# Weights' parts ahead of what is traced behind them, selection paced by VectorE's queue, recurrence spread, branch sums and keys in swapped tiles

## The chip, the cores and the metric

The kernel runs on one core of a Trainium2 chip. The metric is the device time of one execution in microseconds (us). Engines are called PE (TensorE, matrix products), ACT (ScalarE), DVE (VectorE), POOL (GpSimd) and SP (SyncE, which issues the weight loads).

## The reference, cut to what matters

Two layers work on 512 tokens of width 1024. All arithmetic is float32. One layer:

```python
h = rms_norm(x, g_pre_mix); proj = h @ w_in
q, k, v, qi, ki, wi, xr, gr, zu, zv, gate_logits = jnp.split(proj, offsets, axis=-1)
# rope on q, k, qi, ki
y_a = dsa_attention(q, k, v, qi, ki, wi)      # scores of an indexer, top_k = 128 keys a query, softmax
y_b = rg_lru(causal_depthwise_conv(xr, conv_w, conv_b), ...) * jax.nn.gelu(gr)
y_c = chunked_spatial_gating(jax.nn.gelu(zu), rms_norm(jax.nn.gelu(zv), g_gmlp_v), w_spatial, b_spatial)
branch = jnp.einsum('nbsw,nwd->nbsd', jnp.stack([y_a, y_b, y_c]), w_branch)
merged = jnp.einsum('bsnd,nbsd->bsd', jax.nn.sigmoid(gate_logits), branch)
x = x + rms_norm(merged @ w_out, g_post_mix)
f = jnp.square(jax.nn.relu(rms_norm(x, g_pre_ffn) @ w_ffn_up)) @ w_ffn_down
x = x + rms_norm(f, g_post_ffn)
ple = (p_i @ w_ple) * jax.nn.sigmoid(x @ w_ple_gate)
x = x + rms_norm(ple, g_post_ple)
```

In `rg_lru`, with r and i sigmoids of block products of the input: `a = exp(-8 r softplus(-lambda))`, the input is `sqrt(1 - a*a) * (i * x)`, and the state is the scan `h[t] = a[t] h[t-1] + input[t]`.

## The kernel before

Everything is kept as [128 partitions x 512 tokens] tiles, features on the partitions. A float32 product is made of three passes: each operand is split into a high part (`hi`, `xh`, `wh`) and the rest (`lo`, `xl`, `wl`), and PE adds hi*hi, lo*hi and hi*lo (`mm3`, `gemm` at L306 with its matmuls on L313 to L315). A product over 1024 features is 8 x 3 matmuls of 512 columns.

The weights stream through the core in 512 KB blocks. `prep()` (L233) takes the next block: SP loads it into `wr` (three buffers), ACT casts it to `wh` (L244), DVE subtracts to get `wl` (L245). `wh` and `wl` have four buffers each, and `getw()` runs `prep()` three blocks ahead of the product. The second half of a product done in halves (`gemm_halves`) calls `prep()` itself after each eviction. `gemm_arriving` (matmuls on L371) multiplies while the normalised activations are still being made: `x_tiles` makes them tile by tile, with a scaling (L496 or L498), an addition to the residual `X` (L499, on DVE or POOL in turn), the high part `xh` on ACT (L509) and `xl` on DVE (L519). `Stats` gathers squares (L407 on ACT, L413 on POOL), PE sums them (L423), DVE and POOL make the reciprocal root (L442, L443) and PE spreads it (L449). At the very start DVE and ACT also make the tables of the rotary embedding (L133 to L161, one sine on L154), which PE transposes (L164).

Each engine works through its instructions in order. The order within an engine is set by a scheduler at build time from the order in which the code emits them, from the data dependences, and from order-only edges that the code adds. A model clock (`clk`, advanced by `tick()` after each matmul triple) decides when deferred pieces and tasks are emitted. Tasks are generators in queues: selection (`idxq`), recurrence (`recq`), attention (`attq`). `behind_products(fn)` ties what `fn` emits behind the last matmul emitted so far.

In the stretch of the gate logits and branch products (about 150 to 240 us in layer 1, 1050 to 1145 in layer 2) four things share DVE: the weights' `wl`, the selection rounds (`select`, L724: MAX on L730, MATCH_REPLACE on L732, 16 rounds for each block of queries, then a threshold on L736 to L744), the recurrence (L876: Exp L881, Tanh L882, a square on POOL L884, a product on DVE L885, Sqrt L890, products on POOL L893 and L896, the scan L895) and the gates (L853 on DVE, the Tanh L854 on ACT) with the branch sums (L913, L915, L916). The sums `MA` lie in slots M0 to M7, which earlier hold recurrence inputs (`GG`, `XC`), and the keys `KK` lie in the big slots K0 and K1.

Of the kernel before, what the change touches and what calls it, by code (L numbers as in the profile page):

```python
# [8 lines left out]
F32 = mybir.dt.float32  # L9
F32R = mybir.dt.float32r  # L10
# [3 lines left out]
ALU = mybir.AluOpType  # L14
# [36 lines left out]
def hybrid_block_kernel(ctx, tc, xT, pT, pos, vec, bsp, freq, w_in, w_tok, w_lru, w_sp, w_br, w_out, w_up, w_dn, w_ple, w_gate, out, depth=DEPTH, dbg=None):  # L51
# [40 lines left out]
    PICK = 1.7  # L92
    WARM = 120
# [139 lines left out]
    def prep():  # L233
        i = nprep[0]
        nprep[0] += 1
        key, src = order[i]
        raw = wp.tile([128, 1024], F32, tag="wr", name=nm("wr"), bufs=3)
        nc.sync.dma_start(raw, src)
        if key[0] == "sp":
            r3 = raw.rearrange("p (g t) -> p g t", g=8)  # L240
            G.affine_select(out=r3, in_=r3, compare_op=ALU.is_ge, fill=0.0, base=0, pattern=[[0, 8], [1, 128]], channel_multiplier=-1)
        hi = wp.tile([128, 1024], F32R, tag="wh", name=nm("wh"), bufs=NWB)
        lo = wp.tile([128, 1024], F32R, tag="wl", name=nm("wl"), bufs=NWB)
        A.copy(hi, raw)  # L244
        V.tensor_sub(lo, raw, f32v(hi))  # L245
        prepared[key] = (hi, lo)

# [31 lines left out]

    def run_later(force=False):  # L280
        while later:
            later.sort(key=lambda e: e[:2])
            if not force and later[0][0] > clk[0]:
                return
            later.pop(0)[2]()
# [15 lines left out]
    def tick(us):  # L301
        clk[0] += us
        run_later()
        run_tasks()
# [244 lines left out]
    for l in range(depth):  # L549
# [174 lines left out]
        def select(t, sc):  # L724
# [3 lines left out]
            for r in range(TOPK // 8):  # L728
                m8 = small(8, "m8", 4)
                V.max(m8, (sc if r == 0 else wk)[:, :n])  # L730
                if r < TOPK // 8 - 1:
                    V.match_replace(wk[:, :n], m8, (sc if r == 0 else wk)[:, :n], -3.0e38)  # L732
                yield 0.8 + 1.1 * t
# [127 lines left out]
        for j in range(4):  # L861
# [7 lines left out]
            r, i = tmp(), tmp()  # L869
# [8 lines left out]
        def recurrence():  # L878
            for j in range(4):
                a, s = slot(f"B{j}"), slot(f"B{4 + j}")  # L880
                A.activation(a, Rg[j], AF.Exp, scale=nsp8[:, j:j + 1])  # L881
                A.activation(s, Rg[j], AF.Tanh, scale=sp8[:, j:j + 1])  # L882
                q = tmp()
                G.tensor_mul(q, a, a)  # L884
                V.scalar_tensor_tensor(s, q, 1.0, s, op0=ALU.add, op1=ALU.mult)  # L885
                AS.append((a, s))
                yield 1.5
            yield 3.0
            for j in range(4):
                A.activation(AS[j][1], AS[j][1], AF.Sqrt)  # L890
            for j in range(4):
                a, s = AS[j]
                G.tensor_mul(s, s, XC[j][0])  # L893
                hh = tmp()
                V.tensor_tensor_scan(hh, a, s, 0.0, ALU.mult, ALU.add)  # L895
                G.tensor_mul(hh, hh, GG[j])  # L896
                yh, yl = slot(f"B{j}", F32R), slot(f"B{4 + j}", F32R)
                split(hh, yh, yl)
                YB.append((yh, yl))
                yield 4.0  # L900
# [5 lines left out]
        MA = [None] * 8  # L906

        def branch(n, d, w, y, th):
            ps = bank()
            gemm(ps, w, y, 4, c0=(d % 2) * 128)  # L910
            if n == 2:
                MA[d] = slot(f"M{d}")
# [16 lines left out]
        KK = [slot("K0", F32R, True), slot("K1", F32R, True)]  # L929
# [4 lines left out]
        def attention(j):  # L934

            q2, ql = Q[j]
            kk = KK[0][:, j], KK[1][:, j]
# [97 lines left out]
        for j in range(4):  # L1035
# [12 lines left out]
            turn_later(TURN, lambda f=rope(proj(f"k{j}")), j=j: stacked(f, KK[0][:, j], KK[1][:, j]))  # L1048
# [7 lines left out]
        mh = [slot("K0", F32R, True), slot("K1", F32R, True)]  # L1056
        ml = [slot("V0", F32R, True), slot("V1", F32R, True)]
        M = []
        for d in range(8):
# [3 lines left out]
            hi, lo = mh[d // 4][:, d % 4], ml[d // 4][:, d % 4]  # L1063
# [4 lines left out]
        Y = [slot(f"M{d}") for d in range(8)]  # L1068
# [190 lines left out]
```

## Time and profile before

| | |
|---|---|
| median of 3 runs | 1830.21 us (1828.61 to 1830.43) |
| the profiled execution | 1830.5 us, span 1828.8 us, mean granted clock 0.994 |
| busy: PE, DVE, ACT, POOL | 1793.8, 1169.1, 796.0, 364.4 us |
| PE waits: for `wl` in products, for `xl` in arriving products | 10.5 us (6 times), 8.0 us (9 times) |
| L244 casts, L245 subtractions | 303 each, mean 1050 and 1275 ns |

A matmul of 512 columns starts 0.227 us after the one before it when nothing is awaited, though its record lasts 0.39 us, because its end is modelled. The granted clock is given as a share of the full one. Idle time is put down to the instruction that ended it.

### The profile page before, as it was taken

The numbers are of one execution on the slowest core, as the hardware profiler recorded it, in microseconds if no ns is written. First come the engines' busy times: TensorE is split into PE (matmuls) and PEld (weight loads), VectorE is DVE, ScalarE is ACT, GpSimd is POOL, SyncE is SP. The second block draws the span as 40 slices with busy tenths as digits, with TensorE's granted clock in tenths as the row PEclk, the third lists the DMA queues.
The fourth block names the chain that finished last, engine by engine and source line by source line (L and its number), as shares of the span: only waits on it lengthen the run. The fifth ranks groups of instructions, "written<-read, shape, count | busy, mean of one in ns | idle before, by whom it ended". The sixth has DMA issues, their size and how long they took to land.

```text
span 1828.8 us, 22863 instructions
## 1 busy us (share of the span) xinstructions
PE 1793.8 (98%) x8798; PEld 1503.6 (82%) x8798; DVE 1169.1 (64%) x1939; ACT 796.0 (44%) x1288; POOL 364.4 (20%) x292
## 2 busy tenths in 40 slices
PE   8999999999999999999999999999999999999997
PEld 7887788888888888888888877888889888888886
DVE  6888997756385253533687989977564753544345
ACT  5556336654443232223546463465544432222233
POOL 3513222300230000003455141232004100000033
PEclk9999999999999999999999999999999999999998
DMA  5312322222222232332222223222222322223321
GB/s 163 100 68 87 106 95 82 69 93 81 93 86 100 92 104 92 104 104 92 88 72 102 73 83 99 99 86 70 81 93 81 104 93 95 102 92 104 104 81 58
DMA packets 49678, 167.77 MB, mean 92 GB/s; under 512 B 6048, under 2 KB 8864, under 8 KB 49568
## 3 DMA queue, kind: packets, MB, share of 16 engines
q1 hardware_dynamic: 47376, 163.64, 26.7%
q10 hardware_dynamic: 2192, 2.67, 0.4%
q8 instruction: 69, 1.13, 0.3%
q14 instruction: 41, 0.34, 0.1%
HBM read 164.19 MB, written 2.10 MB: 91 GB/s over the span
## 4 chain that ended last, share of the span: by engine, by line
PE 84%; DVE 7%; issue 3%; POOL 3%; ACT 3%; DMA 0%; SPq 0%; ACTq 0%; POOLq 0%; DVEq 0%
PE ps L313 24%; PE ps L315 24%; PE ps L314 24%; PE ps L606 5%; PE ps L371 4%; DVE wl L245 1%; PE ps L983 1%; DVE tmp L732 1%; PE ps L969 1%; DVE m L730 1%; PE ps L697 1%; POOL sacc L413 1%; POOL X L499 1%; DVE xl L519 1%; PE ps L683 1%
## 5 line engine op out<-in xcount | busy, mean ns | idle before, releaser
L244 ACT CAST wh<-wr 128x1024 fp32r<-128x1024 f32 x303 | 317.9, 1050 | 464.8 <-PE ps L315 380.8
L314 PE MATMUL ps<-xh,wl 128*128 128x512 f32 (+1 forms) x1296 | 496.8, 383 | 10.5 <-DVE wl L245 10.5
L245 DVE TENSOR_TENSOR wl<-wr,wh 128x1024 fp32r<-128x1024 f32 x303 | 385.6, 1275 | 185.8 <-ACT wh L244 185.4
L313 PE MATMUL ps<-xh,wh 128*128 128x512 f32 (+1 forms) x1296 | 503.6, 389 | 0.0
L315 PE MATMUL ps<-xl,wh 128*128 128x512 f32 (+1 forms) x1296 | 496.7, 383 | 0.0
L314 PEld LDWEIGHTS ps<-xh,wl 128*128 128x128 f32 x1296 | 244.8, 189 | 56.5 <-DVE wl L245 13.0
L413 POOL TENSOR_TENSOR sacc<-sacc,tmp 128x256 f32<-128x256 f32 (+1 forms) x99 | 108.4, 1096 | 895.8 <-issue 584.5
L315 PEld LDWEIGHTS ps<-xl,wh 128*128 128x128 f32 x1296 | 244.3, 189 | 48.2
L313 PEld LDWEIGHTS ps<-xh,wh 128*128 128x128 f32 x1296 | 244.5, 189 | 46.0 <-issue 1.9
L315 PE MATMUL ps<-V,wh 128*128 128x512 f32 (+1 forms) x528 | 195.4, 370 | 0.0
L313 PE MATMUL ps<-K,wh 128*128 128x512 f32 (+1 forms) x432 | 158.2, 366 | 0.0
L314 PE MATMUL ps<-K,wl 128*128 128x512 f32 (+1 forms) x432 | 157.8, 365 | 0.0
L315 PE MATMUL ps<-B,wh 128*128 128x512 f32 x336 | 131.0, 390 | 0.0
L313 PE MATMUL ps<-A,wh 128*128 128x512 f32 x320 | 125.0, 391 | 0.2 <-ACT A L384 0.2
L314 PE MATMUL ps<-A,wl 128*128 128x512 f32 x320 | 124.6, 389 | 0.0
L1118 DVE TENSOR_TENSOR M<-M,ps 128x512 f32<-128x512 f32 x48 | 33.0, 688 | 141.1 <-PE ps L315 141.1
L1106 DVE TENSOR_TENSOR tmp<-ps,R 128x512 f32<-128x512 f32 x64 | 43.8, 690 | 111.1 <-PE ps L315 109.8
L315 PEld LDWEIGHTS ps<-V,wh 128*128 128x128 f32 x528 | 99.5, 188 | 16.9
L371 PE MATMUL ps<-xl,wh 128*128 128x256 f32 (+1 forms) x264 | 87.2, 330 | 8.5 <-DVE xl L519 8.0
L313 PEld LDWEIGHTS ps<-K,wh 128*128 128x128 f32 x432 | 81.4, 189 | 13.2
L314 PEld LDWEIGHTS ps<-K,wl 128*128 128x128 f32 x432 | 81.5, 189 | 13.1
L371 PE MATMUL ps<-xh,wh 128*128 128x256 f32 (+1 forms) x264 | 85.6, 324 | 1.4 <-ACT xh L509 1.3
(235 smaller groups left out, 2729.1 us busy)
## 6 DMA issues: line engine op xcount, KB each, us to landing
wr<-in_w_in_dram SPq DMA_DIRECT2D x95, 512.0 KB, 3.3
wr<-in_w_up_dram SPq DMA_DIRECT2D x64, 512.0 KB, 3.3
wr<-in_w_dn_dram SPq DMA_DIRECT2D x64, 512.0 KB, 3.3
wr<-in_w_br_dram SPq DMA_DIRECT2D x24, 512.0 KB, 3.3
wr<-in_w_tok_dram SPq DMA_DIRECT2D x16, 512.0 KB, 3.3
wr<-in_w_out_dram SPq DMA_DIRECT2D x16, 512.0 KB, 3.3
wr<-in_w_gate_dram SPq DMA_DIRECT2D x16, 512.0 KB, 3.3
X<-in_xT_dram SPq DMA_DIRECT2D x8, 256.0 KB, 5.4
```

The lines of the kernel that those rows point to most:

```text
L244: A.copy(hi, raw)
L245: V.tensor_sub(lo, raw, f32v(hi))
L313: PE.matmul(ps, wh, xh, start=start, stop=False)
L314: PE.matmul(ps, wl, xh, start=False, stop=False)
L315: PE.matmul(ps, wh, xl, start=False, stop=stop)
L371: PE.matmul(pss[o][:, r], (h3, l3, h3)[m][:, q], xs[q][m // 2][:, r], start=q == 0 and m == 0, stop=q == KT - 1 and m == 2)
L413: G.tensor_add(sacc[:, r], sacc[:, r], self.q[r.start, r.stop])
L499: (G if d in on_g else V).tensor_add(X[d][:, r], X[d][:, r], ys[d][:, r])
L519: V.scalar_tensor_tensor(lo, x, g[:, d:d + 1], f32v(hi), op0=ALU.mult, op1=ALU.subtract)
L606: PE.matmul(ps, x, w, start=k == 0 and i == 0, stop=k == KT - 1 and i == 2)
L1106: V.tensor_mul(t, ps, R)
L1118: V.tensor_add(F[d], F[d], ps)
```

## The change

It has four parts. (1) `weights_first()` runs at the head of each `prep()`: every ACT and DVE instruction emitted since the last `prep()` gets an order-only edge behind that `prep()`'s last cast and last subtraction. (2) A selection round no longer yields a fixed time; `count()` keeps an account of DVE's queue from the sizes of the emitted instructions, and a round is emitted when `vector_free()` finds the queue empty at the model clock. (3) The recurrence makes the Tanh before the Exp, which works in place in the B slots; the square goes from POOL to ACT; square roots, scans and the final splits are tied behind products and spread by longer yields. (4) The branch sums go to the big slots K0 and K1, the keys to M0 to M7, the merged high parts to the M slots, and Y to K0 and K1.

```diff
--- before.py
+++ after.py
@@ -90,6 +90,7 @@
     ATT = 13
     TURN = 7
     PICK = 1.7
+    SLACK = 0.3
     WARM = 120
     FIRST = [0, 1, 4]
 
@@ -231,6 +232,7 @@
     nget = [0]
 
     def prep():
+        weights_first()
         i = nprep[0]
         nprep[0] += 1
         key, src = order[i]
@@ -244,6 +246,21 @@
         A.copy(hi, raw)
         V.tensor_sub(lo, raw, f32v(hi))
         prepared[key] = (hi, lo)
+        ins = nc.cur_bb.bb.instructions
+        parts[:] = [len(ins)] + [next(i.name for i in reversed(ins) if i.engine == e) for e in ENG]
+
+    ENG = (mybir.EngineType.Activation, mybir.EngineType.DVE)
+    parts = []
+
+    def weights_first():
+
+        if not parts:
+            return
+        for i in nc.cur_bb.bb.instructions[parts[0]:]:
+            for e, name in zip(ENG, parts[1:]):
+                if i.engine == e:
+                    tc.add_manual_dep(i, name, mybir.DependencyInfo(mybir.DependencyClass.NoSync, mybir.DependencyReason.SCHED_ONLY), reason="weights first")
+        parts.clear()
 
     def getw(key, ahead=LA):
         assert order[nget[0]][0] == key, (order[nget[0]][0], key)
@@ -276,6 +293,26 @@
 
     def turn_later(us, fn):
         defer(us, lambda: behind_products(fn))
+
+    dve = [0.0, 0]
+
+    def vector_free():
+
+
+        count()
+        return dve[0] <= clk[0] + SLACK
+
+    def count():
+        ins = nc.cur_bb.bb.instructions
+        for i in ins[dve[1]:]:
+            n = 1
+            for _, c in (list(i.outs[0].ap)[1:] if i.outs and hasattr(i.outs[0], "ap") else ()):
+                n *= c
+            if i.engine == mybir.EngineType.DVE:
+                dve[0] = max(dve[0], clk[0]) + 0.08 + n * 0.00118
+            elif i.engine == mybir.EngineType.Pool:
+                dve[0] = max(dve[0], clk[0]) + n * 0.0012
+        dve[1] = len(ins)
 
     def run_later(force=False):
         while later:
@@ -299,6 +336,7 @@
                         q["act"].remove(a)
 
     def tick(us):
+        count()
         clk[0] += us
         run_later()
         run_tasks()
@@ -730,7 +768,9 @@
                 V.max(m8, (sc if r == 0 else wk)[:, :n])
                 if r < TOPK // 8 - 1:
                     V.match_replace(wk[:, :n], m8, (sc if r == 0 else wk)[:, :n], -3.0e38)
-                yield 0.8 + 1.1 * t
+                yield 0.6
+                while not vector_free():
+                    yield 0.3
             thr = m8[:, 7:8]
             gt, cnt = tmp(), small(1, "cnt", 4)
             V.tensor_scalar(gt[:, :n], sc[:, :n], thr, None, op0=ALU.is_gt, op1=ALU.add, accum_out=cnt)
@@ -866,7 +906,7 @@
             pr, pi = bank(), bank()
             mm3(pr, w3[0][:, j], w3[1][:, j], xh, xl, True, True)
             mm3(pi, w3[0][:, 4 + j], w3[1][:, 4 + j], xh, xl, True, True)
-            r, i = tmp(), tmp()
+            r, i = slot(f"B{j}"), tmp()
             A.activation(r, pr, AF.Sigmoid, bias=col(V_BA + j))
             A.activation(i, pi, AF.Sigmoid, bias=col(V_BX + j))
             G.tensor_mul(xc, xc, i)
@@ -877,39 +917,51 @@
 
         def recurrence():
             for j in range(4):
-                a, s = slot(f"B{j}"), slot(f"B{4 + j}")
-                A.activation(a, Rg[j], AF.Exp, scale=nsp8[:, j:j + 1])
-                A.activation(s, Rg[j], AF.Tanh, scale=sp8[:, j:j + 1])
+                a, s = Rg[j], slot(f"B{4 + j}")
+                A.activation(s, a, AF.Tanh, scale=sp8[:, j:j + 1])
+                A.activation(a, a, AF.Exp, scale=nsp8[:, j:j + 1])
                 q = tmp()
-                G.tensor_mul(q, a, a)
+                A.activation(q, a, AF.Square)
                 V.scalar_tensor_tensor(s, q, 1.0, s, op0=ALU.add, op1=ALU.mult)
                 AS.append((a, s))
-                yield 1.5
+                yield 2.5
             yield 3.0
-            for j in range(4):
-                A.activation(AS[j][1], AS[j][1], AF.Sqrt)
+
+            def roots():
+                for j in range(4):
+                    A.activation(AS[j][1], AS[j][1], AF.Sqrt)
+
+            behind_products(roots)
+            yield 3.0
             for j in range(4):
                 a, s = AS[j]
                 G.tensor_mul(s, s, XC[j][0])
+                yield 3.0
                 hh = tmp()
-                V.tensor_tensor_scan(hh, a, s, 0.0, ALU.mult, ALU.add)
-                G.tensor_mul(hh, hh, GG[j])
+
+                def scan(hh=hh, a=a, s=s, j=j):
+                    V.tensor_tensor_scan(hh, a, s, 0.0, ALU.mult, ALU.add)
+                    G.tensor_mul(hh, hh, GG[j])
+
+                behind_products(scan)
                 yh, yl = slot(f"B{j}", F32R), slot(f"B{4 + j}", F32R)
-                split(hh, yh, yl)
                 YB.append((yh, yl))
-                yield 4.0
+                turn_later(5.0, lambda hh=hh, yh=yh, yl=yl: split(hh, yh, yl))
+                yield 5.0
 
         recq = {"wait": [recurrence()], "act": [], "max": 1}
         queues.append(recq)
 
 
-        MA = [None] * 8
+        MA, MB = [None] * 8, []
 
         def branch(n, d, w, y, th):
             ps = bank()
             gemm(ps, w, y, 4, c0=(d % 2) * 128)
             if n == 2:
-                MA[d] = slot(f"M{d}")
+                if d % 4 == 0:
+                    MB.append(slot(f"K{d // 4}", F32, True))
+                MA[d] = MB[d // 4][:, d % 4]
                 V.scalar_tensor_tensor(MA[d], th, 1.0, ps, op0=ALU.add, op1=ALU.mult)
             else:
                 V.scalar_tensor_tensor(th, th, 1.0, ps, op0=ALU.add, op1=ALU.mult)
@@ -926,7 +978,7 @@
         finish(recq)
 
 
-        KK = [slot("K0", F32R, True), slot("K1", F32R, True)]
+        KK = [[slot(f"M{4 * s + j}", F32R) for j in range(4)] for s in range(2)]
 
         VV = [slot("V0", F32R, True), slot("V1", F32R, True)]
         Q, YA = [], [None] * 4
@@ -934,7 +986,7 @@
         def attention(j):
 
             q2, ql = Q[j]
-            kk = KK[0][:, j], KK[1][:, j]
+            kk = KK[0][j], KK[1][j]
             vv = VV[j // 2]
             L = {}
 
@@ -1045,7 +1097,7 @@
 
             turn_later(TURN, q_split)
             Q.append((q2, ql))
-            turn_later(TURN, lambda f=rope(proj(f"k{j}")), j=j: stacked(f, KK[0][:, j], KK[1][:, j]))
+            turn_later(TURN, lambda f=rope(proj(f"k{j}")), j=j: stacked(f, KK[0][j], KK[1][j]))
             if j == 0:
                 finish(idxq)
             defer(ATT, lambda j=j: add_task(attq, attention(j)))
@@ -1053,19 +1105,19 @@
 
         TH = [gate(0, d) for d in range(8)]
         finish(attq)
-        mh = [slot("K0", F32R, True), slot("K1", F32R, True)]
         ml = [slot("V0", F32R, True), slot("V1", F32R, True)]
         M = []
         for d in range(8):
             if d % 2 == 0:
                 w = getw(("br", l, 0, d // 2))
             branch(0, d, w, YA, TH[d])
-            hi, lo = mh[d // 4][:, d % 4], ml[d // 4][:, d % 4]
+            hi, lo = slot(f"M{d}", F32R), ml[d // 4][:, d % 4]
             split(MA[d], hi, lo, scale=0.5)
             M.append((hi, lo))
 
 
-        Y = [slot(f"M{d}") for d in range(8)]
+        yb = [slot("K0", F32, True), slot("K1", F32, True)]
+        Y = [yb[d // 4][:, d % 4] for d in range(8)]
         st = Stats()
         st2 = Stats()
 
```

The lines of the file move with it: L245 becomes L247, L496 and L499 become L534 and L537, L519 becomes L557, L730 and L732 become L768 and L770, L885 becomes L925.

The order of DVE at the start of the program, before and then with the change. `wl_413` to `wl_482` are the first four weights after the first product, `tmp_436` to `tmp_466` the rope tables, `xl_27` the last of the first activations:

```order
L160 TENSOR_SCALAR tmp_466<-tmp_436 128x4x8
L161 COPY tmp_466<-tmp_436 128x4x8
L245 TENSOR_TENSOR wl_422<-wr_419,wh_421 128x1024
L245 TENSOR_TENSOR wl_431<-wr_428,wh_430 128x1024
L245 TENSOR_TENSOR wl_482<-wr_479,wh_481 128x1024
L442 TENSOR_SCALAR sm_502<-ps_497 128x4
```

```order
L557 SCALAR_TENSOR_TENSOR xl_27_252<-X_233,vec_79,xh_26_251 128x512
L247 TENSOR_TENSOR wl_413<-wr_410,wh_412 128x1024
L247 TENSOR_TENSOR wl_422<-wr_419,wh_421 128x1024
L247 TENSOR_TENSOR wl_431<-wr_428,wh_430 128x1024
L134 CAST sm_434<-posi 128x4
L247 TENSOR_TENSOR wl_482<-wr_479,wh_481 128x1024
L139 TENSOR_TENSOR tmp_436<-sm_434,fq 128x32
L159 MEMSET tmp_446 128x512
```

The table instructions, which ended ahead of `wl_422`, now begin behind `wl_482`.

The order of DVE at the boundary from the mix to the feed-forward part of layer 1, before and then with the change. The three `wl` are the first weights of the feed-forward product; the other lines are those of `x_tiles`, and `sm` is a variance:

```order
L245 TENSOR_TENSOR wl_4534<-wr_4531,wh_4533 128x1024
L496 TENSOR_TENSOR M_866_4220<-M_866_4220,ps_4553 128x256
L499 TENSOR_TENSOR X_226<-X_226,M_866_4220 128x256
L496 TENSOR_TENSOR M_867_4221<-M_867_4221,ps_4553 128x256
L245 TENSOR_TENSOR wl_4572<-wr_4569,wh_4571 128x1024
L519 SCALAR_TENSOR_TENSOR xl_13_238<-X_226,vec_79,xh_12_237 128x256
L496 TENSOR_TENSOR M_868_4222<-M_868_4222,ps_4553 128x256
L499 TENSOR_TENSOR X_228<-X_228,M_868_4222 128x256
L519 SCALAR_TENSOR_TENSOR xl_15_240<-X_227,vec_79,xh_14_239 128x256
L496 TENSOR_TENSOR M_869_4223<-M_869_4223,ps_4553 128x256
L245 TENSOR_TENSOR wl_4607<-wr_4604,wh_4606 128x1024
L442 TENSOR_SCALAR sm_4656<-ps_4653 128x2
```

```order
L247 TENSOR_TENSOR wl_4530<-wr_4527,wh_4529 128x1024
L247 TENSOR_TENSOR wl_4568<-wr_4565,wh_4567 128x1024
L247 TENSOR_TENSOR wl_4603<-wr_4600,wh_4602 128x1024
L534 TENSOR_TENSOR K_872_4222<-K_872_4222,ps_4549 128x256
L537 TENSOR_TENSOR X_226<-X_226,K_872_4222 128x256
```

The subtractions stood between the tiles and now stand ahead of the first one; ACT's casts stand ahead of its `xh` likewise.

The order of DVE in the gate stretch of layer 1, around the `wl` that PE waits for at 177 us (`wl_1707` before, `wl_1708` with the change):

```order
L885 SCALAR_TENSOR_TENSOR B_341_1683<-tmp_1686,B_341_1683 128x512
L730 MAX m_357_1732<-tmp_1678 128x8
L732 MATCH_REPLACE tmp_1678<-m_357_1732,tmp_1678 128x384
L885 SCALAR_TENSOR_TENSOR B_355_1720<-tmp_1723,B_355_1720 128x512
L730 MAX m_363_1761<-tmp_1678 128x8
L885 SCALAR_TENSOR_TENSOR B_359_1739<-tmp_1742,B_359_1739 128x512
L853 TENSOR_TENSOR tmp_1751<-ps_1691,R_284 128x512
L732 MATCH_REPLACE tmp_1678<-m_363_1761,tmp_1678 128x384
L730 MAX m_372_1800<-tmp_1678 128x8
L732 MATCH_REPLACE tmp_1678<-m_372_1800,tmp_1678 128x384
L245 TENSOR_TENSOR wl_1707<-wr_1704,wh_1706 128x1024
```

```order
L965 SCALAR_TENSOR_TENSOR K_342_1690<-tmp_1626,ps_1662 128x512
L770 MATCH_REPLACE tmp_1658<-m_340_1681,tmp_1658 128x384
L247 TENSOR_TENSOR wl_1702<-wr_1699,wh_1701 128x1024
L768 MAX m_341_1687<-tmp_1658 128x8
L925 SCALAR_TENSOR_TENSOR B_338_1669<-tmp_1672,B_338_1669 128x512
L770 MATCH_REPLACE tmp_1658<-m_341_1687,tmp_1658 128x384
L247 TENSOR_TENSOR wl_1708<-wr_1705,wh_1707 128x1024
L893 TENSOR_TENSOR tmp_1747<-ps_1692,R_284 128x512
L925 SCALAR_TENSOR_TENSOR B_353_1714<-tmp_1717,B_353_1714 128x512
L925 SCALAR_TENSOR_TENSOR B_355_1732<-tmp_1735,B_355_1732 128x512
```

Between the weight before it and that subtraction stood three recurrence products, a gate product and six selection instructions; now one recurrence product and two selection instructions stand there.

## Rows read from the trace of the kernel before

**Rows 1.** The page, part 1: busy time, share of the span, instructions.

```profile
PE 1793.8 (98%) x8798; PEld 1503.6 (82%) x8798; DVE 1169.1 (64%) x1939; ACT 796.0 (44%) x1288; POOL 364.4 (20%) x292
```

**Rows 2.** PE in time, 177 to 185 us: start, duration, instruction, [idle <-releaser].

```profile
177.16 0.39 PE L313 MATMUL ps<-xh,wh 128*128 128x512 f32 x1
180.82 0.79 PE L314 MATMUL ps<-xh,wl 128*128 128x512 f32 x1 [3.28 <-DVE wl L245]
...
184.27 0.39 PE L313 MATMUL ps<-xh,wh 128*128 128x512 f32 x1
```

**Rows 3.** PE's waits, 170:225, then 1075:1125 us: total, times, longest.

```profile
PE ps L314 <- DVE wl L245: 5.3, 3, 3.3
...
PE ps L314 <- DVE wl L245: 5.1, 3, 3.2
```

**Rows 4.** Windows: busy time (instructions) of PE, PEld, DVE, ACT, POOL; clock, DMA.

```profile
180.80:184.10 3.30, 3.28 (x8) 2.60 (x9) 2.97 (x6) 3.28 (x5) 2.12 (x2) 0.50 0.53 161
1084.20:1088.40 4.20, 4.20 (x12) 3.36 (x13) 3.87 (x6) 4.19 (x6) 3.06 (x3) 0.62 0.39 125
912.00:935.10 23.10, 19.57 (x140) 17.15 (x139) 20.62 (x42) 12.74 (x32) 17.97 (x21) 1.00 0.14 48
```

**Rows 5.** DVE in time, 176 to 181 us.

```profile
179.55 1.22 DVE L245 TENSOR_TENSOR wl<-wr,wh 128x1024 fp32r<-128x1024 f32 x1
```

**Rows 6.** ACT in time, 170 to 176 us.

```profile
172.35 1.03 ACT L244 CAST wh<-wr 128x1024 fp32r<-128x1024 f32 x1
```

**Rows 7.** Line L885, both layers: duration ns min/median/max, first and last start.

```profile
L885 DVE SCALAR_TENSOR_TENSOR B<-tmp,B x8: 666/1589/1768, 168.3 to 1080.0; 128x512 f32<-128x512 f32 x8
```

**Rows 8.** DVE in time, 24 to 36 us.

```profile
24.19 0.18 DVE L138 TENSOR_TENSOR tmp<-sm,fq 128x32 f32<-128x32 f32 x1
24.42 0.48 DVE L158 MEMSET tmp<- 128x512 f32 x1
...
27.16 0.25 DVE L147 TENSOR_SCALAR tmp<-tmp 128x32 f32<-128x32 f32 x2
...
29.33 0.18 DVE L161 COPY tmp<-tmp 128x32 f32<-128x32 f32 x1
32.16 2.36 DVE L245 TENSOR_TENSOR wl<-wr,wh 128x1024 fp32r<-128x1024 f32 x2 [2.66 <-ACT wh L244]
35.02 1.23 DVE L245 TENSOR_TENSOR wl<-wr,wh 128x1024 fp32r<-128x1024 f32 x1 [0.50 <-ACT wh L244]
```

**Rows 9.** ACT in time, 31 to 35 us.

```profile
31.08 2.00 ACT L244 CAST wh<-wr 128x1024 fp32r<-128x1024 f32 x2 [2.27 <-issue]
...
33.94 1.05 ACT L244 CAST wh<-wr 128x1024 fp32r<-128x1024 f32 x1
```

**Rows 10.** PE in time, 32 to 33 us.

```profile
32.20 1.03 PE L164 MATMUL ps<-ident,tmp 128*128 128x128 f32 x8
```

**Rows 11.** DVE in time, 496 to 504 us.

```profile
496.86 0.41 DVE L496 TENSOR_TENSOR M<-M,ps 128x256 f32<-128x256 f32 x1
...
502.16 1.71 DVE L245 TENSOR_TENSOR wl<-wr,wh 128x1024 fp32r<-128x1024 f32 x1
```

**Rows 12.** ACT in time, 500 to 502 us.

```profile
500.60 1.05 ACT L244 CAST wh<-wr 128x1024 fp32r<-128x1024 f32 x1
```

**Rows 13.** PE in time, 499 to 527 us.

```profile
499.76 0.28 PE L371 MATMUL ps<-xh,wh 128*128 128x256 f32 x1
...
526.24 0.48 PE L313 MATMUL ps<-xh,wh 128*128 128x512 f32 x1
```

**Rows 14.** PE's waits, 495 to 527 us: total, times, longest.

```profile
PE ps L371 <- DVE xl L519: 0.9, 2, 0.5
PE ps L371 <- DVE wl L245: 0.4, 1, 0.4
```

**Rows 15.** DVE in time, 908 to 910 us.

```profile
908.99 0.47 DVE L498 SCALAR_TENSOR_TENSOR B<-B,gp,ps 128x256 f32<-128x256 f32 x1
```

**Rows 16.** ACT in time, 912 to 914 us.

```profile
912.73 1.04 ACT L244 CAST wh<-wr 128x1024 fp32r<-128x1024 f32 x1
```

## The prediction

> **What bounds the kernel now.** I read the page first: TensorE (PE) is busy for 98% of the span [rows 1], so the end moves only where PE stands idle or runs slowly. The next view was PE's waits by stretch. In the gate and branch stretch of each layer PE waits three times for the low half `wl` of a weight, 5.3 us in layer 1 and 5.1 us in layer 2 [rows 3]. PE's timeline shows the worst of these: after the matmul at 177.16 us the next starts at 180.82, and the eight starts up to 184.27 come 0.43 us apart where 0.23 is usual [rows 2]. The windows give the clock there: 0.50, the 1.2 GHz level, directly after that idle, and 0.62 over the matching window of layer 2 [rows 4].
>
> Why is `wl` late? Its cast on ScalarE (ACT) ends at 172.35 + 1.03 = 173.4 us [rows 6], but VectorE (DVE) makes the subtraction only at 179.55 [rows 5]. DVE was not waiting for the weight. It worked through selection rounds, recurrence steps and a gate product that stood ahead of it, which is the third order excerpt above. So DVE's order sets this stall, and the change rewrites exactly that order.
>
> **What the stall costs today.** A stall costs its idle time, plus 0.16 us because a 0.39 us record is followed by the next start after 0.23, plus about 0.1 us on the next matmul. Layer 1: 5.3 + 3 x 0.16 + 0.2 for idle, and for the low clock eight starts in 3.45 us instead of 8 x 0.227 = 1.82, so 1.6. That is 7.6 us. Layer 2: 5.1 + 0.7, and twelve starts in 4.20 us instead of 2.72, so 1.5; together 7.3 [rows 2 to 4]. **The most that can be won here is 15 us.**
>
> **Part 1, weights first, in the gate stretch.** In the new order nothing of the selection or the recurrence stands between cast and subtraction except what DVE is already doing. Cast to 173.4, then even behind the longest recurrence product, 1.77 us [rows 7], the subtraction of 1.22 [rows 5] ends at 176.4; PE wants it at 177.16 + 0.23 = 177.4. The stall and its low clock go. The same work still has to be done by DVE, only later, so what is late next would be a subtraction that waits on its cast while a searched block is owed. I charge 0.75 us per layer for that, between 0 (everything on time) and 3 (about the two smaller stalls of a layer kept). Gain: 15.0 - 1.5 = **13.5 us**.
>
> **Parts 2 to 4.** Pacing the selection by an account of DVE's queue changes when rounds are emitted, not how many. The eight squares that move from POOL to ACT and the table loads that fall from 24 to 18 lie on engines that PE does not wait for here, and ACT is 44% busy [rows 1]. Storing the branch sums in other tiles takes away waits of DVE, not work. I cost all of it at nothing by itself: what covers it is the margin of 1 us or more computed above, and if that is gone the charge of 0.75 grows towards 3. One thing is worth a number. The recurrence product L885 takes 0.67 us at best and 1.59 in the median [rows 7], the long ones beside a square on POOL. With the squares on ACT, 4 x (1.59 - 0.67) = 3.7 us of DVE time per layer come free. The page "SBUF — State Buffer" of the Trainium skill, section "SBUF: two separate sides", says that a VectorE instruction with two SBUF inputs and a GpSimd instruction that reads SBUF exclude each other for a whole instruction. By that rule the 3.7 us are really won; without it none would be; the sum stays the same and only the chance of the third rival below falls.
>
> **Part 1 again, where it was not needed: the start.** The rule holds for every weight. In the new order DVE makes four subtractions before it begins the rope tables; before, it did the tables first (first order excerpt). Two of the casts of these weights run at 31.08 to 33.08 [rows 9] and not sooner; I take it that their buffers come free only as PE finishes the first product. The fourth cast, 1.05 us long [rows 9], follows at 33.1 at the earliest. Two subtractions take 32.16 to 34.5 [rows 8], the fourth another 1.2, to 35.7. Only now come the table instructions. They took 0.18 + 0.48 + 0.25 + 0.48 for the head (two memsets among them) and from 27.16 to 29.51 for the rest with the sine [rows 8], 3.7 us; overlaps take off 0.1 and the first table is ready 0.3 before the second. PE's eight transposes of the tables, at 32.20 today [rows 10] and in the same place of PE's order, can start at 35.7 + 3.7 - 0.4 = 39.0. **PE stands 6.8 us** where it stood none. An idle time of 3.3 us was followed by the 1.2 GHz level in layer 1 [rows 2, 4], so I add the same 1.6. Loss **8.4 us**; bounds 5 (casts 2 us sooner and the clock kept) and 9.
>
> **The boundary from mix to feed-forward, in both layers.** Here a weight is cast after each half-product. Before, DVE slipped the normalised activations between the subtractions, beginning at 496.86 [rows 11]. Now all three subtractions precede the first of them (second order excerpt). The third cast cannot run before 500.60 [rows 12], since it follows the eviction of the last half-product. It ends at 501.65, its subtraction at 502.9, so the activations start **6.0 us later**. The first one needs 1.4 us (scale, add, high part) before PE can start: 504.3 instead of 499.76 [rows 13]. From there PE has the same work, 526.24 - 499.76 = 26.5 us [rows 13] less the waits of this stretch, 1.3 [rows 14], and 0.5 for their edges: 24.7. That ends at 529.0, and with 1.6 for the low clock after 4.3 us of idle at 530.6. Loss **4.4 us** each, 8.8 for two. Bounds: 2.4 (DVE's total work decides and the activations catch up) and 6.0 (all of the delay stays).
>
> **The boundary between the layers.** The same shape once: third cast at 912.73 to 913.77 [rows 16], subtraction to 915.0, activations from 915.0 instead of 908.99 [rows 15]. But here PE is fed by DVE anyway: in the 23.1 us after 912 PE is busy for 19.57 and DVE for 20.62 [rows 4], so a permutation of DVE's work costs less than the delay. I take half, **3.0 us**; bounds 0 and 6.
>
> **The sum.** The profiled execution took 1830.5 us (span 1828.8), 0.3 above the median of 1830.2. 1830.5 - 13.5 + 8.4 + 8.8 + 3.0 = 1837.2, so **1837 us**, slower by 0.4%. About 0.2%, 3.7 us, is what a measurement of this kernel can tell from no change: 1826.5 to 1833.9 counts as the same.
>
> **Rivals.**
> *The boundaries hide their delay.* At the three boundaries the products could be bound by DVE's total of work, which the order does not change. Then they cost about 0, and 1830.5 - 13.5 + 8.4 = 1825 us: faster. For it speaks the stretch after 912, where DVE is the busier engine [rows 4]. Against it: in the stretch from 495 PE waits only 1.3 us in all [rows 14], so PE has no slack there to take up a start 4.5 us later. It decides once the three boundaries together cost less than about 1 us. Chance 0.14.
> *The rope tables come in time.* If the buffers of the first weights are free some 5 us earlier, the subtractions end before PE needs the tables; without that loss the sum is 1829 us, no change. Against it: the casts at 31.08 began with no weight missing, after 2.27 us of standing [rows 9], and the buffers depend on PE's matmuls, which the change leaves in place. Chance 0.11.
> *The gate stretch is not relieved.* DVE is nearly full there, and with weights first the postponed searches could end late enough to hold attention or a later subtraction. Half of the gain gone: 1837 + 7 = 1844 us. For it: DVE is busy 2.97 of 3.30 us even in the slow-clock window [rows 4]. Against it: the 3.7 us of L885. Chance 0.15; without those 3.7 us I would give it 0.25.
> That the edges don't take effect is ruled out by the new order itself; the rest, 0.60, is the forecast.
>
> **How the numbers follow.** The forecast's own parts spread by about 5 us to either side, so of its 0.60 some 0.47 lies above 1833.9, 0.12 within the band and 0.01 below. The first rival is split 0.11 faster and 0.03 same, the second 0.04 faster, 0.06 same and 0.01 slower, the third is all slower. Slower: 0.47 + 0.01 + 0.15 = 0.63; same: 0.12 + 0.03 + 0.06 = 0.21; faster: 0.01 + 0.11 + 0.04 = 0.16. The range reaches down into the first rival and up through the third: 1825 to 1845 us; the forecast's own would be 1831 to 1843.
>
> **What the profile after would show.** Right: PE's waits for `wl` in the two gate stretches near zero and the clock full there; one wait of PE of some 6 to 7 us at the table transposes, with the clock at one half after it; in each layer a wait of about 4 us for the first activation of the feed-forward product. Wrong: tables ready near 32 us, PE waits below 1 us at the boundaries, or waits for `wl` still of 1 us and more in the gate stretch.

## The result, and the profile after

| | before | after |
|---|---|---|
| median of 4 runs | 1830.32 us | 1847.18 us (1846.62 to 1847.73) |
| profiled execution, its span | 1830.5, 1828.8 us | 1846.62, 1844.9 us |
| PE busy, mean granted clock | 1793.8 us, 0.994 | 1801.9 us, 0.989 |

The change makes the kernel slower by 0.96%: ratio 1.0096, 95% interval 1.0084 to 1.0108. The direction and most of the places were forecast, but not the size: 1837 us was said, and 1847.2 lies above the range. One execution of run 4 below took 2167.6 us at a granted clock of 0.776 and is left out; in all others the clock is 0.98 or higher. This is what PE waited for after the change, over the whole span (total us, times, longest):

```profile
PE ps L409 <- ACT xh L547: 14.4, 5, 4.4
PE ps L165 <- DVE tmp L162: 6.6, 1, 6.6
PE ps L409 <- DVE xl L557: 3.9, 3, 2.7
PE ps L487 <- POOL rt L481: 2.6, 2, 1.4
...
PE ps L721 <- DVE M L705: 1.4, 2, 1.1
PE ps L644 <- DVE wl L247: 1.3, 2, 0.8
```

The six waits for `wl` in the gate stretches [rows 3] are gone there; L644 is the token product behind them, with 1.3 us in layer 1. New are the rope tables (L165, 6.6 us), the first activations at the three boundaries (L409 for `xh`, the longest 4.4 us), and the first key products (L721).

To see where each microsecond went I compared the start of the same-numbered matmul in both traces; both programs make 8798. "Forecast" is the term of the prediction. The rows of the gate stretch contain the token product behind it.

| stage (matmul numbers) | after minus before, us | forecast |
|---|---|---|
| first products (to 190) | -2.2 | 0 |
| rope tables (190 to 860) | +9.2 | +8.4 |
| gate stretch, layer 1 (860 to 1150) | -5.4 | -6.75 |
| attention, layer 1 (1150 to 2425) | +1.4 | 0 |
| mix to feed-forward, layer 1 (2425 to 2670) | +6.5 | +4.4 |
| boundary between the layers (4150 to 4600) | +4.5 | +3.0 |
| gate stretch, layer 2 (5237 to 5620) | -7.4 | -6.75 |
| attention, layer 2 (5620 to 6780) | +4.9 | 0 |
| mix to feed-forward, layer 2 (6780 to 7000) | +4.8 | +4.4 |
| sum | +16.3 | +6.7 |

**The rope tables.** PE, then DVE, then ACT around 30 us:

```profile
36.82 1.94 PE L165 MATMUL ps<-ident,tmp 128*128 128x128 f32 x8 [6.65 <-DVE tmp L162]
...
38.98 0.63 PE L352 MATMUL ps<-xh,wl 128*128 128x512 f32 x1
39.41 0.63 PE L353 MATMUL ps<-xl,wh 128*128 128x512 f32 x1
```

```profile
29.94 2.36 DVE L247 TENSOR_TENSOR wl<-wr,wh 128x1024 fp32r<-128x1024 f32 x2 [4.23 <-ACT wh L246]
...
32.28 1.22 DVE L247 TENSOR_TENSOR wl<-wr,wh 128x1024 fp32r<-128x1024 f32 x1
33.42 0.18 DVE L139 TENSOR_TENSOR tmp<-sm,fq 128x32 f32<-128x32 f32 x1
...
36.84 0.18 DVE L162 COPY tmp<-tmp 128x32 f32<-128x32 f32 x1
```

```profile
28.85 2.94 ACT L246 CAST wh<-wr 128x1024 fp32r<-128x1024 f32 x3 [7.73 <-PE ps L409]
```

The casts start when PE frees the buffers, as was taken from [rows 9]; they and the arriving products come 2.2 us sooner than in the trace of before. The fourth subtraction ends at 33.5, the tables need until 37.0, and PE stands 6.65 us. Its transposes take 1.94 us instead of 1.03 [rows 10], and from 38.98 on the starts come 0.43 us apart: from 36.8 to 41.5 us the granted clock is 0.50.

**Mix to feed-forward, layer 1.** DVE, POOL and PE:

```profile
504.64 1.22 DVE L247 TENSOR_TENSOR wl<-wr,wh 128x1024 fp32r<-128x1024 f32 x1 [1.65 <-ACT wh L246]
505.78 0.41 DVE L534 TENSOR_TENSOR K<-K,ps 128x256 f32<-128x256 f32 x1
...
513.47 0.16 DVE L480 TENSOR_SCALAR sm<-ps 128x2 f32<-128x2 f32 x1
```

```profile
514.52 0.89 POOL L481 TENSOR_TENSOR rt<-sm,mhalf 128x2 f32<-128x2 f32 x1
```

```profile
507.25 0.58 PE L409 MATMUL ps<-xh,wh 128*128 128x256 f32 x1 [4.36 <-ACT xh L547]
```

The third subtraction precedes the first tile (L534), as in the second order excerpt. PE starts its first arriving product 7.5 us later than before [rows 13], of which 4.4 us are this stall. The variance (L480) now stands behind all tiles of the first half, so POOL makes the root only at 514.52 and PE waits 1.4 us more for it (in L487); the prediction did not count that.

**The keys of layer 2.** PE's timeline, the window behind it (columns as in [rows 4]) and DVE:

```profile
1183.18 0.41 PE L721 MATMUL ps<-M,A 128*128 128x384 f32 x1 [1.08 <-DVE M L705]
1183.90 0.87 PE L721 MATMUL ps<-M,A 128*128 128x384 f32 x3 [0.31 <-DVE M L705]
...
1185.31 0.80 PE L351 MATMUL ps<-B,wh 128*128 128x512 f32 x1
```

```profile
1185.30:1188.80 3.50, 3.50 (x10) 2.78 (x9) 3.50 (x8) 1.72 (x4) 2.20 (x1) 0.52 0.53 159
```

```profile
1181.09 1.23 DVE L247 TENSOR_TENSOR wl<-wr,wh 128x1024 fp32r<-128x1024 f32 x1 [0.19 <-ACT wh L246]
1182.35 1.40 DVE L705 TENSOR_TENSOR M<-tmp,M 64x512 fp32r<-64x512 f32 x2
```

The key tiles `M` (L705) are finished 1.4 us too late, and the clock is at 0.52 for the next 3.5 us. The prediction had no term for this. The wait and the low clock make 3.5 of the 4.9 us that attention loses in layer 2 (by matmul 5660). The other 1.4 us there and the 1.4 us of layer 1 are not the keys: from matmul 1150 to 2425 PE idles for 0.24 us both before and after. In these stretches PE changes between products and attention matmuls 119 and 118 times instead of 109 and 108, as in runs 2 and 4, whose edges reach there too (117 to 119), and in no other run. That this is the cause is not shown.

### The profile page after: what moved, and what is told of

Same layout as the page of the kernel before. It is cut to its first block, busy times and chain, and to the rows that moved or that the text cites. A ratio compares the mean times of both kernels' runs of the same rounds, so it can differ in the third digit from the quotient of the medians.

```text
span 1844.9 us, 22854 instructions
## 1 busy us (share of the span) xinstructions
PE 1801.9 (98%) x8798; PEld 1509.2 (82%) x8798; DVE 1152.2 (62%) x1939; ACT 790.2 (43%) x1290; POOL 348.8 (19%) x284
## 4 chain that ended last, share of the span: by engine, by line
PE 59%; DVE 7%; issue 2%; ACT 1%; POOL 1%; ACTq 0%; POOLq 0%; DVEq 0%
PE ps L351 17%; PE ps L353 17%; PE ps L352 17%; PE ps L409 4%; DVE tmp L770 1%; PE ps L644 1%; DVE wl L247 1%; DVE m L768 1%; PE ps L1035 1%; PE ps L1021 0%; PE ps L461 0%; DVE tmp L846 0%; ACT wh L246 0%; POOL X L537 0%; PE ps L735 0%
## 5 line engine op out<-in xcount | busy, mean ns | idle before, releaser
L247 DVE TENSOR_TENSOR wl<-wr,wh 128x1024 fp32r<-128x1024 f32 x303 | 377.8, 1249 | 226.3 <-ACT wh L246 225.6
L451 POOL TENSOR_TENSOR sacc<-sacc,tmp 128x256 f32<-128x256 f32 (+1 forms) x99 | 108.5, 1096 | 896.6 <-issue 582.7
L409 PE MATMUL ps<-xh,wh 128*128 128x256 f32 (+1 forms) x264 | 89.4, 338 | 14.4 <-ACT xh L547 14.4
L351 PE MATMUL ps<-K,wh 128*128 128x512 f32 x256 | 99.6, 389 | 0.0
L352 PE MATMUL ps<-K,wl 128*128 128x512 f32 x256 | 99.6, 389 | 0.0
L409 PE MATMUL ps<-xl,wh 128*128 128x256 f32 (+1 forms) x264 | 89.3, 338 | 5.1 <-DVE xl L557 3.9
L409 PE MATMUL ps<-xh,wl 128*128 128x256 f32 (+1 forms) x264 | 87.8, 333 | 0.0
L353 PEld LDWEIGHTS ps<-B,wh 128*128 128x128 f32 x336 | 63.5, 189 | 13.6
```

The source lines that it names most:

```text
L351: PE.matmul(ps, wh, xh, start=start, stop=False)
L352: PE.matmul(ps, wl, xh, start=False, stop=False)
L353: PE.matmul(ps, wh, xl, start=False, stop=stop)
L409: PE.matmul(pss[o][:, r], (h3, l3, h3)[m][:, q], xs[q][m // 2][:, r], start=q == 0 and m == 0, stop=q == KT - 1 and m == 2)
L451: G.tensor_add(sacc[:, r], sacc[:, r], self.q[r.start, r.stop])
```

## The experiments

### 1. The edges: without them, alone, only in the gate stretch, not at the start

The runs are numbered in the order in which their labels count. The edits of runs 1, 3 and 4 in `weights_first()` of the changed kernel:

```diff
-        if not parts:
+        if True:
             return
```

```diff
-        if not parts:
+        key = order[nprep[0] - 1][0]
+        mine = key[0] in ("lru", "sp") or key[0] == "in" and key[2][:2] in ("zu", "gr", "g2") or key[0] == "br" and key[2] == 2 or key[0] == "tok" and key[2] == 0
+        if not parts or not mine:
+            parts.clear()
             return
```

```diff
-        if not parts:
+        if not parts or nprep[0] <= 7:
+            parts.clear()
             return
```

Run 2 is the kernel before with `weights_first()`, `parts` and `ENG` added and nothing else.

> Parts 2 to 4 of the change without the order-only edges of part 1. Theory (the edges cause every loss outside the gate stretch): the waits at the rope tables (6.6 us after the change), at the three activation boundaries (4.4, 4.1, 4.4 us) and at the first key products of layer 2 (1.4 us and its half clock) are all gone, and the time is between 1817 us (parts 2 to 4 alone relieve the gate stretch) and 1831 us (the edges alone do). Rival (the swapped tiles cause the loss in attention): PE still waits about 1 us for the keys M and the time is some 4 us above that.

Measured: 1820.89 us, ratio to before 0.9953 (0.9938 to 0.9968). The waits for tables, boundaries and keys are gone; PE's waits (total, times, longest):

```profile
PE ps L409 <- DVE xl L557: 8.0, 9, 3.8
PE ps L644 <- DVE wl L247: 4.5, 2, 2.4
...
PE ps L352 <- DVE wl L247: 1.3, 2, 1.0
PE ps L409 <- ACT xh L547: 0.8, 1, 0.8
```

The two gate stretches gain 7.75 and 7.74 us up to the token product, exactly as with the edges. Behind that point they lose 2.4 and 4.3 us without the edges, 2.3 and 0.3 us with them. **So the edges win nothing in the gate stretch proper and 4.0 us in the token product of layer 2 and the first product after it; in all they cost 26 us.**

> The kernel before with part 1 alone. Theory: the same waits at the rope tables (6 to 7 us) and the boundaries (about 4 us each) as after the change, 1830 + 7 + 3 x 5 = 1852 us less what the edges win in the gate stretch; if the edges alone win its 15 us, 1837 us, if parts 2 to 4 are needed for it, 1845 to 1852 us. Rival (losses come from the four parts together): close to 1830 us with waits at the boundaries below 1 us.

Measured: 1874.09 us, ratio 1.0247 (1.023 to 1.0264), worse than either end of the forecast. PE's waits:

```profile
PE ps L387 <- ACT xh L525: 13.6, 4, 4.4
PE ps L329 <- ACT wh L245: 10.3, 2, 5.2
PE ps L329 <- DVE tmp L869: 8.5, 2, 4.2
PE ps L164 <- DVE tmp L161: 6.6, 1, 6.6
PE ps L330 <- DVE wl L246: 6.1, 2, 3.1
```

The tables' wait is the same 6.6 us, and the boundaries (L387) wait as after the change. In the gate stretch the old recurrence now stands ahead of later casts, and two waits of 5.2 and 3.1 us a layer take the place of the three of before, and the stretch as a whole loses 2 to 3 us (10.0 and 10.7 lost in its first part, 7.75 won in the second, by the numbered matmuls). The three old waits are gone, but PE also comes there 10 us later, so on balance the edges alone do not relieve the stretch. What the forecast lacked besides is attention, which loses 7.9 and 7.5 us; 4.2 us of each are a wait for the gate product L869.

> The whole change, but the edges only behind weights of the gate stretch (those of zu, spatial, gr, recurrence, third gate and its branch product, second token product). Theory: gain of the gate stretch kept (13 us), all other losses gone: 1816 to 1819 us, faster than before by 0.6 to 0.8%. Rival (the gain needs the edges of other weights too, or other parts lose): 1825 us and more.

Measured: 1820.33 us, ratio 0.9951 (0.9936 to 0.9966), between the two forecasts. All losses at tables and boundaries are gone, but three waits stay, for the keys, in the token product and for an attention tile (L426):

```profile
PE ps L724 <- DVE M L708: 1.4, 2, 1.1
PE ps L647 <- DVE wl L247: 1.3, 2, 0.7
PE ps L354 <- DVE tmp L426: 1.2, 1, 1.2
```

> The whole change without the edges of the first seven weights. Theory: PE's wait at the rope tables falls from 6.6 us to none and its half clock with it, 1847 - 8 = 1839 us, boundaries as after the change. Rival (something else delays the tables): about 1847 us.

Measured: 1836.39 us in one execution, the profiled one, 10 us below the change's; no wait at the tables, and by matmul number that stage costs 0.0. The table's +9.2 is the price of the edges at the start.

### 2. Why the keys are late

> The third run (edges only in the gate stretch) with the two mask instructions that end a selection (1.29 and 1.48 us on POOL at 1150.9 us of that run) on DVE. Theory (in layer 2 the first key products wait because these two stand ahead of the first query's rope products in POOL's queue, by 2.7 us): PE's wait of 1.4 us for the keys M and the half clock behind it go, 1820 - 3 = 1817 us. Rival (the keys wait for the swapped tiles or for DVE): the wait stays, 1820 us or more.

```diff
-            G.tensor_add(gt[:, :n], gt[:, :n], eq[:, :n])
-            G.tensor_scalar(BIAS[t], gt[:, :n], -NEG, NEG, op0=ALU.mult, op1=ALU.add)
+            V.tensor_add(gt[:, :n], gt[:, :n], eq[:, :n])
+            V.tensor_scalar(BIAS[t], gt[:, :n], -NEG, NEG, op0=ALU.mult, op1=ALU.add)
```

Measured: 1820.19 us, ratio 0.9948 (0.9933 to 0.9962), no better, and the wait for the keys grew:

```profile
PE ps L724 <- DVE M L708: 2.2, 2, 1.9
```

This run does not settle the theory, because it puts a delay on DVE in the place of the one on POOL. In the third run the masks (L788, L789) do stand ahead of the query's rope products (L632, L633) on POOL, and DVE then stands idle for 2.65 us:

```profile
1150.88 1.29 POOL L788 TENSOR_TENSOR tmp<-tmp,tmp 128x512 f32<-128x512 f32 x1 [35.34 <-DVE tmp L787]
1152.26 1.48 POOL L789 TENSOR_SCALAR bias<-tmp 128x512 bf16<-128x512 f32 x1
1153.82 1.29 POOL L632 TENSOR_TENSOR tmp<-tmp,tmp 128x512 f32<-128x512 f32 x1
```

```profile
1148.34 1.22 DVE L785 TENSOR_TENSOR_SCAN tmp<-tmp 128x512 f32<-128x512 f32 x1
...
1150.06 0.75 DVE L787 SCALAR_TENSOR_TENSOR tmp<-tmp,cnt,tmp 128x512 f32<-128x512 f32 x1
...
1153.79 0.01 DVE L631 LOAD_MASK_SELECT tmp<-ps  x1
...
1157.17 2.81 DVE L1098 TENSOR_TENSOR tmp<-tmp,A 64x512 fp32r<-64x512 f32 x2 [2.65 <-ACT A L1097]
...
1161.43 1.40 DVE L708 TENSOR_TENSOR M<-tmp,M 64x512 fp32r<-64x512 f32 x2
```

The query's shuffle (L631) was done at 1151.5; its rope product starts on POOL 2.4 us after that, ACT's copy (L1097) waits for POOL, and DVE for ACT. In run 5 POOL is free sooner, but the masks and longer subtractions beside POOL move the key's shuffle on DVE from 1153.79 to 1157.23, and the key tiles come at 1162.50 instead of 1161.43. In both runs the closing steps of the selection (L785, L787 and the masks) fall into the rope work of the first query and key.

> The third run (edges in the gate stretch) with selection rounds at the old fixed times. Theory (pacing brings the end of the selection ahead of the first query's rope work, and that delays the keys): no wait for the keys M in layer 2, 1811 to 1814 us. Rival (the edges do): the wait of 1.4 to 2.2 us with its half clock stays, 1815 us and more.

```diff
-                yield 0.6
-                while not vector_free():
-                    yield 0.3
+                yield 0.8 + 1.1 * t
```

Measured: 1817.16 us, ratio 0.9929 (0.9913 to 0.9946). PE does not wait for the keys at all in layer 2, although the edges are there. The time is above the forecast because the first products took 2.4 us longer than in run 6 (see the last section) and one wait of 1.9 us for an attention tile came in. In run 10 the masks come only at 1163.2 us on POOL, behind the key tiles (1153.9). Run 1 has the pacing without the edges and no wait for the keys either: there the masks begin at 1141.2, ahead of the rope work (1151.1), and three subtractions stand behind the end of the selection. So it takes both: paced rounds, and edges that move these subtractions ahead of the last rounds and the end of the selection into the rope work.

### 3. Which part makes the gain

Runs 6 to 8 are run 1 (no edges) with one more part undone; run 9 is the kernel before with one part added.

> The first run (no edges) with selection rounds at the old fixed times. Theory (pacing keeps DVE's queue short, so that the subtractions in the gate stretch are on time): about half or more of the 7.7 us per layer comes back, 1826 to 1834 us. Rival (the recurrence or the tiles relieve the stretch): within 2 us of 1821.

The edit is the one just shown. Measured: **1812.06 us, ratio 0.9903 (0.9886 to 0.9919), the best of all**, against the theory. PE's waits in the whole span:

```profile
PE ps L409 <- DVE xl L557: 6.9, 9, 2.7
...
PE ps L409 <- DVE wl L247: 0.8, 2, 0.4
```

No wait for a subtraction is left in either gate stretch, and none in the token product. The pacing costs 8.8 us (1820.89 - 1812.06). By matmul number 6.7 of these lie in the token products and the first product behind them; in the two profiled executions another 2.6 us lie in the first products (see the last section). In run 1 the rounds stand in a row on DVE: a subtraction for which PE waits 2.4 us begins only at 1123.39 us behind the rounds before it, and three more follow only behind the last step of the selection:

```profile
1141.08 4.99 DVE L247 TENSOR_TENSOR wl<-wr,wh 128x1024 fp32r<-128x1024 f32 x3
```

> The first run (no edges) with the old recurrence: squares on POOL, roots and scans where they were. Theory (the recurrence is not what relieves the stretch): within 3 us of 1821. Rival (its bunched products and table loads made the worst stall at 177 us): that stall of 3 us and its half clock return in both layers, about 1831 us.

```diff
-            r, i = slot(f"B{j}"), tmp()
+            r, i = tmp(), tmp()
 ...
-                A.activation(q, a, AF.Square)
+                G.tensor_mul(q, a, a)
```

and the rest of `recurrence()` as before. Measured: 1828.51 us, ratio 0.9994 (0.9985 to 1.0003), near the rival's forecast: the gain is gone. Six waits for `wl` are there again, but the worst ones not at the old place. They come 36 matmuls sooner in both layers, with 2.95 and 2.05 us, and the clock is at 0.71 and 0.58 in some 3.7 us behind them. The waits of the whole span, the first stall and DVE ahead of it:

```profile
PE ps L352 <- DVE wl L247: 8.1, 6, 3.0
```

```profile
172.26 0.50 PE L352 MATMUL ps<-xh,wl 128*128 128x512 f32 x1 [2.95 <-DVE wl L247]
```

```profile
166.02 1.51 DVE L925 SCALAR_TENSOR_TENSOR B<-tmp,B 128x512 f32<-128x512 f32 x1 [5.40 <-POOL tmp L924]
```

DVE stands idle for 5.4 us (4.85 in layer 2) because the next instruction in its order is a recurrence product that waits for a square on POOL, and that square stands on POOL behind a product (L912) that waits for ACT. The subtraction, whose cast ended by 166.6, stands behind it and begins only at 170.75.

> The first run (no edges) with branch sums and keys in their old tiles. Theory: DVE waits for POOL again by 0.3 to 0.7 us at three branch sums a layer; PE waits by about as much at most, 1821 to 1824 us. Rival (the tiles make the gain): 1828 us or more.

```diff
-                MA[d] = MB[d // 4][:, d % 4]
+                MA[d] = slot(f"M{d}")
 ...
-        KK = [[slot(f"M{4 * s + j}", F32R) for j in range(4)] for s in range(2)]
+        KK = [slot("K0", F32R, True), slot("K1", F32R, True)]
```

Measured: 1824.28 us, ratio 0.9975 (0.9965 to 0.9985). The old tiles cost 3.4 us with the pacing, at the upper end of the theory. By matmul number they cost more: the two gate stretches with their token products gain 2.1 and 0.2 us, where run 1 gains 5.4 and 3.4. That is 6.5 us, part of which the medians hide: this profiled execution comes out of the first products 3.8 us sooner than run 1's. DVE waits for POOL at the branch sums as the theory has it (3.4 us in eight waits), but PE loses more than these waits, mostly in the token products:

```profile
PE ps L644 <- DVE wl L247: 6.2, 2, 3.2
```

> The kernel before with part 3 alone. Theory (the spread recurrence makes the gain in the gate stretch; the tiles add the branch sums' waits of DVE; pacing only costs): 1812 us with the tiles, so 1813 to 1817 us here, with PE's three waits for a subtraction in each gate stretch gone or below 1 us. Rival (recurrence and tiles work only together): 1824 us and more.

Part 3's `recurrence()` and `r` in the B slots, in the kernel before. Measured: 1816.42 us, ratio 0.9924 (0.9909 to 0.9939). Both gate stretches gain the same 7.75 and 7.74 us. So with rounds at fixed times the tiles matter nothing there, although DVE waits 6.0 us for POOL at the branch sums. One wait of 1.8 us for an attention tile is left that run 6 does not have. Part 3 itself was not taken apart: no run separates the squares on ACT from the fewer table loads (20 instead of 24 here) and from the later roots and scans.

## Why the prediction was right and wrong

- **What bounds the kernel** held in the main: all changes of the time but 2.8 us in attention are waits or a low clock of PE.
- **The start** was right in its mechanism (subtractions, then tables, then transposes) and in its size, 9.2 against 8.4. That the buffers come free only as PE finishes is shown by the casts that moved 2.2 us with it and waited for PE (L409).
- **The boundaries** were right in their mechanism and place; runs 1 and 3, without edges there, lose nothing. The sizes were short, 15.8 against 11.8. In layer 1 the missing 2.1 us are mostly the wait of 1.4 for the variance root, an instruction that the working did not move though the order showed it behind the tiles. "I take half" was too little at the boundary between the layers: the stall there is 4.1 us, as large as at the others.
- **The failed step stands in "Parts 2 to 4": "I cost all of it at nothing by itself".** The working looks at the margin in the gate stretch alone; attention behind it has no term. It lost 6.3 of the 9.6 us that the sum fell short: 3.5 are the keys of layer 2, which wait because pacing and edges together bring the end of the selection into the first query's rope work; for the other 2.8 the cause is open. The boundaries, mis-sized, are 4.0 of the rest, the gate stretches 0.7, and the start with the first products gives 1.4 back.
- **The gate stretch** was forecast well, 12.8 of 13.5 us, but for the wrong reason: the gain was given to part 1. Run 9 has all of it from the recurrence alone, run 1 has it without an edge up to the token product, run 2 with edges alone has none on balance. The right size was luck. The sentence that failed says that the squares "lie on engines that PE does not wait for here": PE waits for DVE, and DVE for POOL. Before, it stood idle for the square, 2.25 us in each layer:

```profile
168.29 1.77 DVE L885 SCALAR_TENSOR_TENSOR B<-tmp,B 128x512 f32<-128x512 f32 x1 [2.25 <-POOL tmp L884]
```

After the change the row of this product reads:

```profile
L925 DVE SCALAR_TENSOR_TENSOR B<-tmp,B x8: 672/684/692, 180.1 to 1096.3; 128x512 f32<-128x512 f32 x8
```

Its median falls from 1.59 us [rows 7] to 0.68. The 3.7 us a layer of the prediction took the median for all four; in sum the eight products fall from 11.2 to 5.5 us, 2.9 us a layer, and in run 9, which has the whole gain, by 2.25. The page "SBUF — State Buffer" of the Trainium skill, section "SBUF: two separate sides", would have such a product excluded by any POOL instruction that reads SBUF. The trace agrees: each product of 1.5 to 1.8 us overlaps POOL instructions and each of 0.67 overlaps none. But it was not the squares alone, as the prediction had it: the third product overlaps L893, and in run 9, with the squares on ACT, the first still takes 1.32 us beside L872. How the gain divides between these shorter products, the vanished wait for the square and the spreading of the rest is not shown.
- **The pacing** was held to change only when rounds are emitted. That was true, and just this cost 8.8 us without the edges and made the keys late with them.
- **The rivals.** The third, that the gate stretch is not relieved, did not come, but a part of what it feared is what happened: the searches end at a time that holds attention, at a price of 3.5 us for the keys. The first and second fell: the boundaries don't hide a late start, and the tables don't come in time.

## What to carry to other kernels

An order rule that is right at one stall is a cost at every place where the work it holds back is what the bottleneck engine needs next; look for those places in the new order before believing the gain. When several edits arrive together, undo each one alone: here one of four takes away every old wait in the gate stretches, and the version with two of them, the recurrence and the tiles, is 1% faster than the kernel before. An engine that works in order passes on the waits of others: before calling an engine uncritical, look at who waits for it, and who waits for that one.

## What was not expected of the hardware

The start of the program varies although the order is the same. In run 1 and run 6 the first wait for an `xl`, by PE's timeline, is

```profile
21.65 0.80 PE L409 MATMUL ps<-xl,wh 128*128 128x512 f32 x1 [3.75 <-DVE xl L557]
```

```profile
20.25 0.50 PE L409 MATMUL ps<-xl,wh 128*128 128x512 f32 x1 [2.65 <-DVE xl L557]
```

The waits differ by 1.1 us, and the 190th matmul comes 2.6 us apart in these two; over the kernels it lies between 0.1 us later and 3.8 us earlier than in the trace of before. The 1.1 us are in the DVE rows just ahead, of run 1 and then of run 6:

```profile
14.76 5.16 DVE L423 TENSOR_TENSOR wl<-wr,wh 128x512 fp32r<-128x512 f32 x3
```

```profile
14.44 4.08 DVE L423 TENSOR_TENSOR wl<-wr,wh 128x512 fp32r<-128x512 f32 x3
```

These are three subtractions beside POOL's sums of squares (L451). In run 1 each takes 1.75 to 1.79 us; in run 6 the second takes 0.68. It begins there at 16.15, within 0.02 us of a sum on POOL, and the four sums from that one on take 6.89 us; in run 1 it begins at 16.46, 0.2 us behind the start of that sum, and the four take 6.45. Whether the order of the two decides was not tried, but the length of one instruction moves the first wait by a microsecond. Differences of 2 to 3 us between two single profiles mean nothing unless the stage is known.

Short idle times were followed by the low clock in one place and not in another. After the change two waits of 1.08 and 0.31 us in layer 2, with short products between them, were followed by the clock of 0.52 shown above. In the kernel before, a single wait of 1.34 us that ended at 200.3 us was followed by a window at full clock:

```profile
200.30:204.00 3.70, 3.68 (x16) 3.07 (x17) 3.31 (x6) 1.57 (x3) 1.29 (x1) 1.00 0.43 142
```

So were the longer single waits of run 1 in the token products, 2.1 and 2.4 us (clock 1.00 in the 3.7 us behind each), while after those of run 8, 3.0 and 3.2 us, it was 0.61 and 0.50. What decides was not tried.
